# First layer's x: parts split straight from the turned banks, the f32 copy made by GpSimd, idle products dropped, raw turns moved

## The chip, the cores and the metric

The kernel runs on one core of one Trainium2 chip. A core has five engines that work side by side, each through its own queue in order: TensorE (PE, with its weight loads PEld), VectorE (DVE), ScalarE (ACT), GpSimd (POOL) and SyncE (SP, which here only issues DMAs). The metric is device microseconds of one execution, median of three runs. Smaller is better.

## The reference

A decoder trunk of two layers over 16 learned meta tokens and 512 tokens (528 columns), model width 1024, all in f32. Layer 0 is gated linear attention, layer 1 differential softmax attention. Cut to what matters here, layer 0 begins with:

```python
h  = concatenate([meta, x])                 # (528, 1024)
hn = rmsnorm(h, g_norm[0])                  # x * rsqrt(mean(x^2) + eps) * g
proj = hn @ w_in                            # 1024 -> 6160 columns
q, k, v, z, g_lr = split(proj, ...)         # g_lr: 16 columns, rank of the gate
lg = log_sigmoid(g_lr @ w_gate_up + b_gate) / 16
# chunked scan over 64-token chunks with decay exp(cumsum(lg)), then rms, silu(z) gate, w_out
h  = h + y
```

The second layer and a last rmsnorm follow. The change touches only the start of layer 0: how `hn` is put into the form that the products read, and the first product with it, `g_lr`.

## The kernel before, in words

**Number format.** Every large product is done on pairs of fp32r tiles: a value is kept as a high part (ACT copies it with rounding to fp32r) and a low part (DVE subtracts the high part from the value). A product is then three products: high by high, high by low, low by high. `split` (line 274) makes such a pair: line 284 (ACT) and line 285 (DVE).

**Layout.** Activations stand turned: the 1024 model columns are 8 groups of 128 partitions, the tokens lie along the free axis (528: 16 meta, then 512). `X["b11"]` and `b12` hold groups 0 to 3 for the first and second 264 tokens, `X["b21"]` and `X["b22"]` groups 4 to 7. Each is a pair of tiles.

**The prologue.** Token blocks (meta, then four of 128) are loaded, squared and summed (ACT), given their factor (DVE, then POOL for the power -0.5), scaled (DVE, line 723) and turned by TensorE (`turned`, line 743). The scaled turns land in eight PSUM banks, `pts[0]` to `pts[7]`, one for each group k, 512 tokens wide: the first four in the banks named bx, bx, bv, by, the other four in banks of the pool ps, which has four in all. `xm` holds the 16 meta columns, turned and already multiplied by the norm's weight `g_sb`. The unscaled x is turned too (`raw_turn`, line 731, into ps banks) and copied by `raw_copy` (ACT line 737, DVE line 739) to `hT`, the residual stream.

**Making x in the kernel before** (`scaled_pair` and the loop behind it): for groups two at a time, ACT (line 801) and DVE (line 802) each copy one whole bank times `g_sb` to an f32 tile `xg` (named y); POOL puts the meta columns there (line 800). Then `split` makes high and low parts from the f32 tile, 528 columns at a time (two groups of 264). Between them stand the splits of the first two weight tiles wanted by the v products (`ws.make_one`, `kept`, lines 281, 282, 284, 285; wh and wl are a weight's high and low part). The f32 tile is needed later: `token_sums` forms sums and differences of its quarters (x1 to x4) for the seven-product scheme that the later heads use.

**The gate's product**: 32 TensorE products (line 1027) with the 112-column stationary tile `glr`, k by k, into two banks `pgs` (named bx). Ahead of the first ones stand idle products (`warm_up`, line 657, ones by ones into a bank nobody reads); among them stand the turns of raw blocks 3, 4 and 0 and pieces of the first v tile (`W.fill`, line 904). Behind it the gate's rows are copied out (ACT 1044, DVE 1047, ACT 1049, DVE 1052), the up-projection weight is split (ACT 1054, DVE 1055), and then `decay(k)` runs eight times: two products (line 1070) that need both, three ACT steps (1071 to 1073), two DVE steps (1076) and a scan (1077). PE goes on with v and q tiles between the decays.

**What sets the order.** PE's order is the order of the code (a manual schedule) throughout. ACT's and DVE's is the code's until `ordered.close()`; behind that a list scheduler with its own costs puts their instructions in order. Waits between engines are set by the framework from what the instructions read and write. Weight tiles (`raw`) come by SP's DMA queue into two buffers; each transfer waits until the tile two before it has been split.

Of the kernel before, what the change touches and what calls it, by code (L numbers as in the profile page):

```python
# [11 lines left out]
F32 = mybir.dt.float32  # L12
# [3 lines left out]
AF = mybir.ActivationFunctionType  # L16
ALU = mybir.AluOpType
# [3 lines left out]
P = 128  # L21
D = 1024
NM = 16
# [194 lines left out]
def trunk(ctx, tc, x, meta, g_norm, gla_w_in, gla_w_gate_up, gla_b_gate, gla_gnorm, gla_w_out,  # L218
# [21 lines left out]
    def T(p, shape, dt, tag, **kw):  # L240
        uid[0] += 1
        return p.tile(shape, dt, tag=tag, name=f"{tag}_{uid[0]}", **kw)

    def pb_tile(tag):
        return T(pb_pool, [P, 512], F32, tag, bufs=2 if tag == "bx" else 1)
# [7 lines left out]
    def ps_tile():  # L253
        return T(ps_pool, [P, 512], F32, "ps")
# [23 lines left out]
    def split(hi, lo, src, scale=None, keep=False):  # L278

        if keep:  # L280
            act.activation(hi, src, AF.Copy)
            kept.append(lambda: dve.tensor_tensor(lo, src, hi.bitcast(F32), op=ALU.subtract))
        elif scale is None:
            act.activation(hi, src, AF.Copy)  # L284
            return dve.tensor_tensor(lo, src, hi.bitcast(F32), op=ALU.subtract)  # L285
        else:
            act.activation(hi, src, AF.Copy, scale=scale)
            return dve.scalar_tensor_tensor(lo, src, scale, hi.bitcast(F32), op0=ALU.mult, op1=ALU.subtract)
# [365 lines left out]
    def warm_up(n, t=None):  # L654
        t = warm if t is None else t
        for _ in range(n):
            pe.matmul(t[:, :P], ones, ones, start=True, stop=True)
# [83 lines left out]
    def turned(b, ks):  # L741
        for k in ks:
            pe.transpose(pts[k][:, (b - 1) * P:b * P], yt[k // 4][:, b - 1, k % 4 * P:(k % 4 + 1) * P], ident)
# [43 lines left out]

    b12 = x_parts(6)
    xg = []

    def scaled_pair(k0):
        i = k0 // 4
        if k0 % 4 == 0:
            if i == 1:
                for kt in range(4, KT):
                    pts.append(ps_tile())
                    for b in range(1, 5):
                        turned(b, [kt])
            xg.append(T(gp, [P, 4, L], F32, f"y{i}"))
            pool.tensor_copy(xg[i][:, :, :NM], xm[:, 4 * i:4 * i + 4, :])  # L800
        act.activation(xg[i][:, k0 % 4, NM:], pts[k0], AF.Copy, scale=g_sb[:, 0, k0:k0 + 1])
        dve.tensor_scalar(xg[i][:, k0 % 4 + 1, NM:], pts[k0 + 1], g_sb[:, 0, k0 + 1:k0 + 2], None, op0=ALU.mult)

    scaled_pair(0)
    for k0 in range(0, KT, 2):
        if k0 + 2 < KT:
            scaled_pair(k0 + 2)
        i, ks = k0 // 4, slice(k0 % 4, k0 % 4 + 2)
        for n, o in enumerate((X[("b11", "b21")[i]], (b12, X["b22"])[i])):
            split(o[0][:, ks, :], o[1][:, ks, :], xg[i][:, ks, n * HT:(n + 1) * HT])  # L810
        if k0 in (0, 4):
            ws.make_one()
        if k0 == 2:
            kept.pop()()
    ws.held = 0
    x1, x2 = xg[0][:, :, :HT], xg[0][:, :, HT:]
    x3, x4 = xg[1][:, :, :HT], xg[1][:, :, HT:]
# [196 lines left out]
    q_gla_v(0, heads[0])  # L1014
    pgs = pb_pair()
    ws.held = 1
    idle = pb_tile("bv")
    turns_of = {(2, 2): (3, 1), (2, 3): (4, 0), (4, 0): (4, 1)}
    for k in range(KT):
        for n in range(2):  # L1020
            for i, x in enumerate((X["b11"], b12) if k < 4 else (X["b21"], X["b22"])):
                if k == 0:
                    warm_up((3, 3, 1, 4)[2 * n + i], idle)
                if (k, 2 * n + i) in turns_of:
                    b, half = turns_of[k, 2 * n + i]
                    raw_turn(b, [half])
                pe.matmul(pgs[i][:112, :HT], glr[:, k, :], x[n][:, k % 4, :],
                          start=k == 0 and n == 0, stop=k == KT - 1 and n == 1)
        if 1 <= k <= 4:
            W.fill(0.6)  # L1030
        if k == 1:
            raw_turn(3, [0])
        if k == 4:
            raw_turn(0)
        if k == 5:
            for b in (3, 4):
                for i in range(2):
                    raw_copy(b, i, act)
            raw_copy(0, 0, dve)
            raw_copy(0, 1, act)  # L1040
    gh = T(gp, [P, L], F32R, "a0")
    halves = [(pg, slice(i * HT, (i + 1) * HT)) for i, pg in enumerate(pgs)]
    for pg, cs in halves:
# [6 lines left out]
    for pg, cs in halves:  # L1050
        with tc.issue_after(low.ins):
            low = dve.tensor_tensor(gs[32:32 + RANK, cs], pg[32:32 + RANK, :HT], gh[32:32 + RANK, cs].bitcast(F32), op=ALU.subtract)
    wur = T(gp, [P, D], F32R, "z")
    high = act.activation(wur, wup, AF.Copy)
    low = dve.tensor_tensor(wur[64:96], wup[64:96], wur[64:96].bitcast(F32), op=ALU.subtract)
# [27 lines left out]
    for k in range(KT):  # L1083
        decay(k)
        if k == KT - 1:

            tc.mark_branch_hint_location("steep", "LikelyTaken", engines=[
                mybir.EngineType.PE, mybir.EngineType.DVE, mybir.EngineType.Activation, mybir.EngineType.SP])
        W.fill(3.5 if k else 2.0)
        if 1 <= k <= 4:  # L1090
            with behind_gate() if k >= 2 else ExitStack():
                token_sums(k - 1)

    eL = T(hp, [P, KT, 5], F32, "eL")
# [940 lines left out]
```

## Time and profile before

| | |
|---|---|
| median of 3 runs | 964.44 us (964.29 to 965.32) |
| the profiled execution's own time | 964.28 us |
| its span | 962.5 us |
| mean granted TensorE clock | 0.998 |
| PE busy | 952.1 us (99%) |
| DVE busy | 797.0 us (83%) |
| ACT busy | 633.9 us (66%) |
| POOL busy | 82.5 us (9%) |

How to read it: a row of the timeline gives the start in us, how long it took, engine, line of the kernel, operation, output from input, shape and how many in a row; in brackets how long the engine had been idle and who ended that. PE's rows overlap: one product is given some 0.28 us from start to end, while the next starts 0.12 us after it. So PE's pace is read from starts. The same holds in a smaller measure on ACT and DVE, where the next may start some 0.1 us before the end of the one ahead.

### The profile page before, as it was taken

The page shows a single profiled execution, that of the slowest core. Times are in us where ns is not written, and L with a number is a line of the kernel's source. Part 1 is how long each engine was busy: PE and PEld are TensorE (multiplying, and loading weights), DVE is VectorE, ACT ScalarE, POOL GpSimd, SP SyncE. Part 2 cuts the span into 40 slices and gives each one's busy share as a digit, 9 for nine tenths or more (in the row PEclk, how much of TensorE's full clock was granted, in tenths as well). Part 3 has the DMA queues.
Part 4 walks back from the last instruction along what each step waited for, and adds up shares of the span by engine and source line. Part 5 has one row for each costly group of instructions (what it writes and reads, how often), then busy time and mean ns, then how long its engine had stood idle before and what let it go on. Part 6 is the DMA issues. An engine that isn't in the chain of part 4 may idle for free.

```text
span 962.5 us, 18493 instructions
## 1 busy us (share of the span) xinstructions
PE 952.1 (99%) x7173; PEld 911.4 (95%) x7173; DVE 797.0 (83%) x1556; ACT 633.9 (66%) x1311; POOL 82.5 (9%) x167
## 2 busy tenths in 40 slices
PE   9999999999999999999999999999999999999997
PEld 8999999999999999998999898999999999989986
DVE  7989986886878787667997897888889889888875
ACT  8776755477647667657657685585776766755673
POOL 1000000000000100000001121111101101110012
PEclk9999999999999999999999999999999999999999
DMA  8322223634362227234348515234252261523312
GB/s 198 89 83 57 88 67 128 139 114 124 125 166 89 88 94 164 64 110 153 99 105 176 133 56 141 86 122 115 72 166 89 79 160 47 147 90 98 110 45 87
DMA packets 128746, 104.96 MB, mean 109 GB/s; under 512 B 51197, under 2 KB 113181, under 8 KB 128656
## 3 DMA queue, kind: packets, MB, share of 16 engines
q1 hardware_dynamic: 123328, 93.80, 35.4%
q10 hardware_dynamic: 5328, 9.95, 2.9%
q8 instruction: 57, 0.93, 0.4%
q14 instruction: 33, 0.27, 0.1%
HBM read 83.64 MB, written 11.80 MB: 99 GB/s over the span
## 4 chain that ended last, share of the span: by engine, by line
PE 83%; DVE 4%; ACT 1%; DMA 1%; issue 1%; POOL 0%; SPq 0%; POOLq 0%; DVEq 0%
PE bx L441 20%; PE bv L441 12%; PE by L441 11%; PE ps L410 8%; PE bx L998 5%; PE bx L431 4%; PE bx L410 3%; PE bv L998 2%; PE by L998 2%; PE ps L1240 2%; PE bv L410 2%; PE by L410 2%; DMA raw<-in_diff_w_in_dram 1%; PE bv L431 1%; PE by L431 1%; PE ps L1876 1%
## 5 line engine op out<-in xcount | busy, mean ns | idle before, releaser
L285 DVE TENSOR_TENSOR wl<-raw,wh 128x1024 fp32r<-128x1024 f32 x93 | 113.6, 1222 | 20.3 <-ACT wh L284 19.6
L284 ACT ACTIVATE wh<-raw 128x1024 fp32r<-128x1024 f32 x93 | 97.9, 1052 | 39.0 <-PE by L998 22.8
L441 PE MATMUL bv<-x,wh 128*128 128x264 f32 (+1 forms) x736 | 108.9, 285 | 0.0
L441 PE MATMUL bx<-x,wh 128*128 128x264 f32 (+1 forms) x720 | 105.5, 285 | 0.0
L441 PEld LDWEIGHTS bv<-x,wh 128*128 128x128 f32 x736 | 96.8, 188 | 0.9 <-DVE z L498 0.3
L441 PEld LDWEIGHTS bx<-x,wh 128*128 128x128 f32 x720 | 94.4, 188 | 0.5
L285 DVE TENSOR_TENSOR wl<-sum,wh 128x1024 fp32r<-128x1024 f32 x46 | 56.2, 1221 | 10.9 <-ACT wh L284 10.7
L1741 ACT ACTIVATE p<-p,st 128x528 f32<-128x528 f32 (+3 forms) x64 | 36.4, 569 | 40.1 <-DVE st L1739 40.1
L441 PE MATMUL bv<-x,wl 128*128 128x264 f32 (+1 forms) x368 | 62.4, 286 | 0.1
L462 ACT ACTIVATE u<-bx 128x264 f32<-128x264 f32 (+1 forms) x128 | 48.4, 378 | 20.3 <-PE bx L441 17.2
L441 PE MATMUL bx<-x,wl 128*128 128x264 f32 (+1 forms) x360 | 59.0, 284 | 0.0
L284 ACT ACTIVATE wh<-sum 128x1024 fp32r<-128x1024 f32 x46 | 48.4, 1052 | 11.1 <-PE bv L441 5.5
L441 PE MATMUL bx<-x,a11h 128*128 128x264 f32 (+1 forms) x360 | 53.0, 285 | 0.0
L441 PE MATMUL by<-x,a12h 128*128 128x264 f32 (+1 forms) x360 | 52.5, 285 | 0.0
L441 PEld LDWEIGHTS bv<-x,wl 128*128 128x128 f32 x368 | 51.5, 188 | 0.4 <-issue 0.3
L284 ACT ACTIVATE a11h<-raw 128x512 fp32r<-128x512 f32 x46 | 28.9, 628 | 33.8 <-DMA raw<-in_diff_w_in_dram 13.5
L441 PEld LDWEIGHTS bx<-x,wl 128*128 128x128 f32 x360 | 50.0, 189 | 0.3 <-DVE wl L285 0.2
L441 PEld LDWEIGHTS bx<-x,a11h 128*128 128x128 f32 x360 | 47.8, 189 | 0.6
L441 PEld LDWEIGHTS by<-x,a12h 128*128 128x128 f32 x360 | 46.9, 188 | 0.0
L1744 POOL TENSOR_TENSOR st<-st,minus 128x1 f32<-128x1 f32 x32 | 21.4, 670 | 277.4 <-ACT p L1741 225.5
L566 POOL TENSOR_TENSOR st<-st,mhalf 128x1 f32<-128x1 f32 (+1 forms) x20 | 12.1, 606 | 370.3 <-DVE st L565 370.3
L441 PE MATMUL by<-x,a22h 128*128 128x264 f32 (+1 forms) x280 | 40.1, 284 | 0.0
(503 smaller groups left out, 2671.5 us busy)
## 6 DMA issues: line engine op xcount, KB each, us to landing
raw<-in_diff_w_in_dram SPq DMA_DIRECT2D x52, 512.0 KB, 4.8
raw<-in_gla_w_in_dram SPq DMA_DIRECT2D x48, 512.0 KB, 4.2
raw<-in_gla_w_out_dram SPq DMA_DIRECT2D x8, 1024.0 KB, 5.7
raw<-in_diff_w_out_dram SPq DMA_DIRECT2D x8, 1024.0 KB, 5.2
raw<-in_diff_w_in_dram SPq DMA_DIRECT2D x6, 1024.0 KB, 5.9
vd<-planes ACTq DMA_DIRECT2D x12, 268.0 KB, 2.1
vd<-keep ACTq DMA_DIRECT2D x12, 264.0 KB, 2.3
T<-bdr SPq DMA_DIRECT2D x8, 264.0 KB, 3.1
```

The source lines that it names most:

```text
L284: act.activation(hi, src, AF.Copy)
L285: return dve.tensor_tensor(lo, src, hi.bitcast(F32), op=ALU.subtract)
L410: pe.matmul(ps, l, r, start=first and n == 0, stop=last and n == 2, **kw)
L431: pe.matmul(bank, a[:, k, :], b[k] if n0 is None else b[k][:, n0 + i * nn:n0 + (i + 1) * nn], start=n == 0 and ks[0] == 0, stop=n == len(t ...
L441: pe.matmul(bank[:, :x[q].shape[2]], w[p][:, k * P:(k + 1) * P], x[q][:, k, :], start=first and i == 0, stop=i == len(PASSES) - 1, skip_gr ...
L462: W.moved = act.activation(t, self.bx[:, :self.n], AF.Copy, scale=self.sc)
L566: pool.tensor_tensor(dst, dst, mhalf[:np_, :dst.shape[1]], op=ALU.pow)
L998: pe.matmul(banks[i][:, :HT], h.t[p][:, k, mm * P:(mm + 1) * P], s.y[q][k][:, i * HT:(i + 1) * HT], start=n == 0, stop=n == len(PASSES) - 1)
L1240: pe.matmul(o, s.kd[:, i, kc], s.qs[:, i, t0:t0 + n], start=i == 0, stop=i == 1)
L1741: act.activation(p[:, :nk], p[:, :nk], AF.Exp, scale=-1.0, bias=st[:, m:m + 1], accum_out=st[:, 2 + m:3 + m])
L1744: pool.tensor_tensor(st[:, 5:6], st[:, 3:4], minus, op=ALU.pow)
L1876: pe.matmul(ps[i], yp[hd][p][:, k, b * P:(b + 1) * P], wt[q][cs.start // 512][:, 2 * hd + k, cs.start % 512:(cs.stop - 1) % 512 + 1], star ...
```

## The change

- `scaled_pair` and the f32 copy from PSUM go. Groups are taken one by one. For each group k and each half n, ACT makes the high part straight from the bank times `g_sb` (line 803 of the changed kernel, 248 columns for n = 0, 264 for n = 1), and DVE the low part from the bank, `g_sb` and that high part (line 804). The meta columns of both halves' first tiles are split from `xm` ahead of that (two small pairs).
- All turns of groups 4 to 7 stand before that.
- The weight splits stand behind group 3 and behind group 7; before, they stood behind the first, second and third pair of groups.
- The f32 tile is made by POOL as high plus low (line 812), four times 128x4x264.
- The gate's products: the eleven idle products go; k = 0 takes its four in another order; one piece of v work (24 products) behind k = 3; raw block 3's turns behind k = 4 and 5; those of blocks 4 and 0 behind all. Block 3's copies stand ahead of the gate's rows, those of blocks 4 and 0 between the gate's rows and the up-projection split.
- `token_sums(0)` gets the same ordering edge (`behind_gate`) as the others.

```diff
     b12 = x_parts(6)
     xg = []
-
-    def scaled_pair(k0):
-        i = k0 // 4
-        if k0 % 4 == 0:
-            if i == 1:
-                for kt in range(4, KT):
-                    pts.append(ps_tile())
-                    for b in range(1, 5):
-                        turned(b, [kt])
-            xg.append(T(gp, [P, 4, L], F32, f"y{i}"))
-            pool.tensor_copy(xg[i][:, :, :NM], xm[:, 4 * i:4 * i + 4, :])
-        act.activation(xg[i][:, k0 % 4, NM:], pts[k0], AF.Copy, scale=g_sb[:, 0, k0:k0 + 1])
-        dve.tensor_scalar(xg[i][:, k0 % 4 + 1, NM:], pts[k0 + 1], g_sb[:, 0, k0 + 1:k0 + 2], None, op0=ALU.mult)
-
-    scaled_pair(0)
-    for k0 in range(0, KT, 2):
-        if k0 + 2 < KT:
-            scaled_pair(k0 + 2)
-        i, ks = k0 // 4, slice(k0 % 4, k0 % 4 + 2)
-        for n, o in enumerate((X[("b11", "b21")[i]], (b12, X["b22"])[i])):
-            split(o[0][:, ks, :], o[1][:, ks, :], xg[i][:, ks, n * HT:(n + 1) * HT])
-        if k0 in (0, 4):
+    for kt in range(4, KT):
+        pts.append(ps_tile())
+        for b in range(1, 5):
+            turned(b, [kt])
+    x_of = [(X["b11"], b12), (X["b21"], X["b22"])]
+    for i in range(2):
+        hi, lo = [t[:, :, :NM] for t in x_of[i][0]]
+        split(hi, lo, xm[:, 4 * i:4 * i + 4, :])
+    for k in range(KT):
+        g = g_sb[:, 0, k:k + 1]
+        for n, x in enumerate(x_of[k // 4]):
+            hi, lo = [t[:, k % 4, NM * (1 - n):] for t in x]
+            src = pts[k][:, HT - NM:] if n else pts[k][:, :HT - NM]
+            act.activation(hi, src, AF.Copy, scale=g)
+            dve.scalar_tensor_tensor(lo, src, g, hi.bitcast(F32), op0=ALU.mult, op1=ALU.subtract)
+        if k == 3:
             ws.make_one()
-        if k0 == 2:
             kept.pop()()
+        if k % 4 == 3:
+            xg.append(T(gp, [P, 4, L], F32, f"y{k // 4}"))
+            for n in (0, 1) if k == 3 else (1, 0):
+                hi, lo = x_of[k // 4][n]
+                pool.tensor_tensor(xg[-1][:, :, n * HT:(n + 1) * HT], hi.bitcast(F32), lo.bitcast(F32), op=ALU.add)
+    ws.make_one()
     ws.held = 0
...
     ws.held = 1
-    idle = pb_tile("bv")
-    turns_of = {(2, 2): (3, 1), (2, 3): (4, 0), (4, 0): (4, 1)}
     for k in range(KT):
-        for n in range(2):
-            for i, x in enumerate((X["b11"], b12) if k < 4 else (X["b21"], X["b22"])):
-                if k == 0:
-                    warm_up((3, 3, 1, 4)[2 * n + i], idle)
-                if (k, 2 * n + i) in turns_of:
-                    b, half = turns_of[k, 2 * n + i]
-                    raw_turn(b, [half])
-                pe.matmul(pgs[i][:112, :HT], glr[:, k, :], x[n][:, k % 4, :],
-                          start=k == 0 and n == 0, stop=k == KT - 1 and n == 1)
-        if 1 <= k <= 4:
-            W.fill(0.6)
-        if k == 1:
-            raw_turn(3, [0])
-        if k == 4:
-            raw_turn(0)
-        if k == 5:
-            for b in (3, 4):
-                for i in range(2):
-                    raw_copy(b, i, act)
-            raw_copy(0, 0, dve)
-            raw_copy(0, 1, act)
+        for i, n in ((0, 0), (0, 1), (1, 0), (1, 1)) if k == 0 else ((0, 0), (1, 0), (0, 1), (1, 1)):
+            pe.matmul(pgs[i][:112, :HT], glr[:, k, :], x_of[k // 4][i][n][:, k % 4, :],
+                      start=k == 0 and n == 0, stop=k == KT - 1 and n == 1)
+        if k == 3:
+            W.fill(2.6)
+        if k in (4, 5):
+            raw_turn(3, [k - 4])
+    for i in range(2):
+        raw_copy(3, i, act)
+    raw_turn(4)
+    raw_turn(0)
     gh = T(gp, [P, L], F32R, "a0")
...
+    for b in (4, 0):
+        raw_copy(b, 0, act if b else dve)
+        raw_copy(b, 1, act)
     wur = T(gp, [P, D], F32R, "z")
...
         if 1 <= k <= 4:
-            with behind_gate() if k >= 2 else ExitStack():
+            with behind_gate():
                 token_sums(k - 1)
```

How the order moves, at the three places of which the prediction speaks. A row is line, operation, output from input and shape; in square brackets the engines whose progress the instruction waits for (`DVE_49` is VectorE's counter, `PE_49` TensorE's, `Activation_49` ScalarE's). In the names, bx_200, bx_201, bv_202 and by_203 are the banks of groups 0 to 3, x_1_77 and x_34_259 the first and second half's x parts, y_35_260 the f32 tile.

ScalarE where x is made, before:

```order
L801 ACTIVATE y_35_260<-bx_200,g_sb 128x512 [waits DVE_49,PE_49]
L801 ACTIVATE y_35_260<-bv_202,g_sb 128x512
L284 ACTIVATE x_1_77<-y_35_260 128x528 [waits DVE_49,Activation_49,Pool_49]
L284 ACTIVATE x_34_259<-y_35_260 128x528
L281 ACTIVATE wh_270<-raw_133 128x1024 [waits DMAHW0_49]
L801 ACTIVATE y_42_293<-ps_273,g_sb 128x512 [waits PE_49]
```

ScalarE at the same place, with the change:

```order
L284 ACTIVATE x_1_77<-t_242 128x4x16 [waits DVE_49]
L284 ACTIVATE x_2_78<-t_242 128x4x16
L803 ACTIVATE x_1_77<-bx_200,g_sb 128x248 [waits PE_49]
L803 ACTIVATE x_34_259<-bx_200,g_sb 128x264 [waits DVE_49]
L803 ACTIVATE x_1_77<-bx_201,g_sb 128x248 [waits PE_49]
L803 ACTIVATE x_34_259<-bx_201,g_sb 128x264 [waits DVE_49]
L803 ACTIVATE x_1_77<-bv_202,g_sb 128x248 [waits PE_49]
L803 ACTIVATE x_34_259<-bv_202,g_sb 128x264 [waits DVE_49]
L803 ACTIVATE x_1_77<-by_203,g_sb 128x248 [waits PE_49]
L803 ACTIVATE x_34_259<-by_203,g_sb 128x264 [waits DVE_49]
L281 ACTIVATE wh_300<-raw_133 128x1024 [waits DMAHW0_49]
```

In each group the second half's high part now waits for VectorE; what it waits for is the low part of the first half, read from the same bank.

VectorE at that place, with the change:

```order
L804 SCALAR_TENSOR_TENSOR x_1_77<-bx_200,g_sb,x_1_77 128x248 [waits Activation_49]
L804 SCALAR_TENSOR_TENSOR x_34_259<-bx_200,g_sb,x_34_259 128x264 [waits Activation_49]
L804 SCALAR_TENSOR_TENSOR x_1_77<-bx_201,g_sb,x_1_77 128x248 [waits Activation_49]
L804 SCALAR_TENSOR_TENSOR x_34_259<-bx_201,g_sb,x_34_259 128x264 [waits Activation_49]
L804 SCALAR_TENSOR_TENSOR x_1_77<-bv_202,g_sb,x_1_77 128x248 [waits Activation_49]
L804 SCALAR_TENSOR_TENSOR x_34_259<-bv_202,g_sb,x_34_259 128x264 [waits Activation_49]
```

Each low part waits for its high part on ScalarE; before, a pair of groups was handed over at once.

ScalarE between the second weight split and the up-projection's, before (wh_308 is the second weight tile's high part, a the gate's rows, z_435 the up-projection weight):

```order
L284 ACTIVATE wh_308<-raw_133 128x1024 [waits DMAHW1_49]
L284 ACTIVATE x_2_78<-y_42_293 128x528 [waits DVE_49,Activation_49]
L284 ACTIVATE x_3_79<-y_42_293 128x528
L737 ACTIVATE hT_90<-ps_346 128x4x128 [waits PE_49]
L737 ACTIVATE hT_90<-ps_353 128x4x128 [waits PE_49]
L737 ACTIVATE hT_90<-ps_359 128x4x128 [waits PE_49]
L737 ACTIVATE hT_90<-ps_381 128x4x128 [waits PE_49]
L737 ACTIVATE hT_90<-ps_401 128x4x16 [waits PE_49]
L1044 ACTIVATE a_20_159<-bx_316 16x264 [waits PE_49]
```

The same stretch with the change:

```order
L284 ACTIVATE wh_326<-raw_133 128x1024 [waits DMAHW1_49]
L737 ACTIVATE hT_90<-ps_378 128x4x128 [waits PE_49]
L737 ACTIVATE hT_90<-ps_387 128x4x128 [waits PE_49]
L1031 ACTIVATE a_20_159<-bx_330 16x264 [waits PE_49]
L1031 ACTIVATE a_20_159<-bx_331 16x264 [waits PE_49]
L1036 ACTIVATE a_55_422<-bx_330 16x264 [waits DVE_49,Activation_49]
L1036 ACTIVATE a_55_422<-bx_331 16x264 [waits DVE_49]
L737 ACTIVATE hT_90<-ps_402 128x4x128 [waits PE_49]
L737 ACTIVATE hT_90<-ps_407 128x4x128 [waits PE_49]
L737 ACTIVATE hT_90<-ps_417 128x4x16 [waits PE_49]
L1044 ACTIVATE z_437<-v_13_122 128x1024 [waits DMAHW5_49,DMAHW6_49,DMAHW4_49,DMAHW7_49,DMAHW1_49,DMAHW0_49]
```

Two of the raw copies stand ahead of the gate's rows and three behind them, ahead of the up-projection split; before, all five stood ahead of the gate's rows.

## The prediction

> **What bounds the kernel now.** I read the page's busy shares and its chain of work first, then PE's waits, then two stretches, then the timeline of the first 42 us engine by engine.
>
> ```profile
> PE 952.1 (99%) x7173; PEld 911.4 (95%) x7173; DVE 797.0 (83%) x1556; ACT 633.9 (66%) x1311; POOL 82.5 (9%) x167
> PE 83%; DVE 4%; ACT 1%; DMA 1%; issue 1%; POOL 0%; SPq 0%; POOLq 0%; DVEq 0%
> ...
> PE bx L904 <- DVE a L1052: 0.3, 1, 0.3
> PE bx L441 <- DVE ks L881: 0.2, 1, 0.2
> ...
> 33.00:60.00 27.00, 27.00 (x223) 26.73 (x223) 24.49 (x35) 23.35 (x50) 0.00 (x0) 1.00 0.28 79
> 60.00:82.00 22.00, 21.85 (x179) 21.43 (x177) 21.58 (x38) 14.28 (x25) 0.00 (x0) 1.00 0.22 67
> ```
>
> PE is the bound: it works in order, from 33 us on almost without a gap (27.00 of 27 us, 21.85 of 22), and its waits in the whole span are a few tenths. So whatever moves PE's place at 33 us moves the end by nearly as much: later idle time is too small to take up a delay. DVE has 2.5 us to spare between 33 and 60 us and next to nothing between 60 and 82.
>
> The place of the change, on PE:
>
> ```profile
> 13.01 0.44 PE L743 MATMUL bx<-ident,y 128*128 128x128 f32 x2 [0.28 <-DVE y L723]
> 13.50 1.91 PE L743 MATMUL ps<-ident,y 128*128 128x128 f32 x16
> 15.24 0.83 PE L657 MATMUL bv<-ones 128*128 128x128 f32 x6
> 27.00 0.28 PE L904 MATMUL bv<-x,wh 128*128 128x264 f32 x1
> 29.92 0.28 PE L904 MATMUL bx<-x,wh 128*128 128x264 f32 x1
> 30.54 2.09 PE L904 MATMUL bx<-x,wh 128*128 128x264 f32 x15 [0.34 <-DVE a L1052]
> 32.71 0.40 PE L1070 MATMUL ps<-a,z 128*128 128x264 f32 x2
> 41.91 0.41 PE L1070 MATMUL ps<-a,z 128*128 128x264 f32 x2
> ...
> L657 PE MATMUL bv<-ones 128*128 128x128 f32 x22 | 3.0, 275 | 0.0
> ```
>
> The last gate products are issued by 27.00, where the v products begin; 24 products take 2.92 us (27.00 to 29.92, 0.1215 each); the next wants the gate's banks and stalls; the first decay is at 32.71, the third at 41.91. ACT and DVE at that place:
>
> ```profile
> 12.06 1.06 ACT L737 ACTIVATE hT<-ps 128x512 f32<-128x512 f32 x2
> 22.42 2.04 ACT L737 ACTIVATE hT<-ps 128x512 f32<-128x512 f32 x4
> 27.08 0.65 ACT L1044 ACTIVATE a<-bx 16x264 fp32r<-16x264 f32 x2 [1.29 <-PE bx L1027]
> 29.32 0.38 ACT L1049 ACTIVATE a<-bx 16x264 fp32r<-16x264 f32 x1 [0.53 <-DVE a L1047]
> 29.73 1.06 ACT L1054 ACTIVATE z<-v 128x1024 fp32r<-128x1024 f32 x1
> ...
> 23.53 1.32 DVE L285 TENSOR_TENSOR x<-y,x 128x528 fp32r<-128x528 f32 x2
> 24.77 1.25 DVE L822 TENSOR_TENSOR y<-y 128x1056 f32<-128x1056 f32 x1
> 27.50 1.79 DVE L1047 CAST a<-bx 16x264 fp32r<-16x264 f32 x4 [1.34 <-ACT a L1044]
> 30.06 0.42 DVE L1052 TENSOR_TENSOR a<-bx,a 16x264 fp32r<-16x264 f32 x1
> 30.82 1.22 DVE L1055 TENSOR_TENSOR z<-v,z 32x1024 fp32r<-32x1024 f32 x1
> 40.90 0.77 DVE L1076 SCALAR_TENSOR_TENSOR t<-ps,t 128x264 f32<-128x264 f32 x2
> ```
>
> Now the last x part is ready at 24.85 (23.53 + 1.32), ahead of PE's need. The gate's rows run 27.08 to 30.48, the up-projection's low part ends at 32.04 and the first decay follows 0.67 later.
>
> **The change part by part.** *Idle products.* 22 pieces go. Sixteen pieces of that size take 13.50 to 15.24, 0.109 each, so 2.4 us of PE; with the stall at 30.54 (0.62 between two starts where 0.12 is normal) PE could win 2.9 us, if x were ready. It is not.
>
> *The split.* In the changed order each group is a relay over one bank: high part of half 0 (ACT), low part (DVE), then ACT's high part of half 1, which waits for DVE, then DVE's low part. Before, each bank had one reader. The prices:
>
> ```profile
> L801 ACT ACTIVATE y<-ps,g_sb 128x512 f32<-128x512 f32 x2 | 1.4, 688 | 0.0
> L737 ACT ACTIVATE hT<-ps 128x512 f32<-128x512 f32 x7 | 3.7, 587 | 0.0
> 31.76 0.39 ACT L951 ACTIVATE t<-bv 128x264 f32<-128x264 f32 x1
> ...
> 61.21 0.43 DVE L881 SCALAR_TENSOR_TENSOR qs<-bv,t 128x264 f32<-128x264 f32 x1
> 61.56 0.42 DVE L881 SCALAR_TENSOR_TENSOR qs<-by,t 128x264 f32<-128x264 f32 x1
> L422 DVE SCALAR_TENSOR_TENSOR vm<-ps,short,vm 32x128 fp32r<-32x128 f32 x8 | 2.6, 339 | 0.2
> L420 DVE TENSOR_TENSOR am<-ps,am 32x128 fp32r<-32x128 f32 x32 | 9.0, 282 | 1.6 <-ACT am L418 0.5
> L282 DVE TENSOR_TENSOR wl<-raw,wh 128x1024 fp32r<-128x1024 f32 x1 | 1.2, 1219 | 0.0
> ```
>
> A scale read from a tile costs ACT 0.10 (688 against 587), so a high part of 264 takes 0.39 + 0.10, near 0.48, and of 248 near 0.465. On DVE it costs 0.06 (339 against 282): 0.48 and 0.465. DVE starts its next one 0.08 before the end of one (61.21 to 61.56 for 0.43). A hand-over costs 0.03 to 0.04: the gate's copies on DVE end at 29.29 (27.50 + 1.79), and ACT, waiting for them, starts at 29.32. One group then takes: low part 0.465, hand-over 0.04, high part 0.48, hand-over 0.035, low part 0.48 less 0.08. Sum **1.43 us a group**. From below, with neither surcharge, 1.21; with twice the hand-over, 1.5. I take 1.43, since the nearest rows have the surcharges.
>
> The Trainium skill speaks against letting both engines read one bank: "PSUM — Partial Sum Buffer", section "PSUM bank collisions raise a hardware error", says that ScalarE and VectorE must not be in one bank at once, two reads included, and that software has to keep them apart. By that rule the relay cannot be loosened; the order's waits on DVE agree, and the sum by it is the one below.
>
> Start: ACT's raw copies end at 13.12; the two small meta parts follow (64 columns, 0.22 each by the nearest row, quoted below, less the overlap of 0.1), so 13.45; the first bank is turned by then (13.01). The first high part ends at 13.92 and the first low part starts at 13.95; DVE's own small parts fit between. The fourth group's last low part starts at 13.95 + 3 x 1.43 + 1.02 = 19.26 and ends at 19.74. Then the weight: ACT 19.13 to 20.19 (1.06), DVE 20.22 to 21.44, free at 21.36; in the relay's rhythm the fifth group would have begun at 19.67, so the weight adds 1.7. The eighth group's last low part starts at 21.36 + 4.29 + 1.02 = 26.67 and ends at **27.15**, 2.3 later than now.
>
> *PE.* It stands at 15.24 with the gate's products and is led by the relay: some 2.9 us idle before 20.1, then 24 v products to 23.04, then the other gate products and block 3's turns as parts come; the last gate product leaves at 27.3. Turns of blocks 4 and 0 now stand behind it: eight at 0.109 and eight small ones, one of them waiting for block 3's copies; PE takes up v work at 28.9 instead of 27.00, +1.9.
>
> *ACT and the gate's rows.* Its last high part ends at 26.64; the weight's high part runs 26.54 to 27.6, block 3's two copies (0.51 each, 2.04 for four) to 28.6. The gate's rows start at 28.5 instead of 27.08, +1.4. Block 4's two copies and the small one then stand ahead of the up-projection: 1.15 more. Its high part starts at 29.73 + 1.4 + 1.15 = 32.3 and the low part ends at 32.04 + 2.5 = **34.55**. The banks come free at about 31.7 and PE wants them at 31.86, so that stall (0.5) goes. PE's 18 products bring it to 34.05; the decay waits till 34.6. First decay: 34.6 against 32.71, **+1.9**.
>
> *Token sums.* The first (1.25 us on DVE at 24.77) now comes behind the gate. From the up-projection's low part to the second decay's DVE steps there stands as much work as before (32.04 to 40.90, 8.86), because another sum moved behind them: they end near 44.15. PE's third decay needs their banks at 41.91 + 1.9 = 43.8: +0.3. The extra 1.25 is then taken up by DVE's 2.5 spare us before 60; without that cover PE would pay it at 78, where it waits for line 881.
>
> *POOL and the DMAs.* The f32 copies:
>
> ```profile
> 955.18 1.28 POOL L1871 TENSOR_TENSOR t<-keep,x 128x512 f32<-128x512 f32 x1 [2.57 <-DVE keep L1863]
> 955.12 0.42 DVE L1863 TENSOR_TENSOR keep<-keep,ps 128x256 f32<-128x256 f32 x1
> 25.57 0.22 ACT L737 ACTIVATE hT<-ps 128x64 f32<-128x64 f32 x1 [1.11 <-PE ps L731]
> 23.64 0.99 SPq L302 DMA_DIRECT2D raw<-in_gla_w_in_dram  x2
> 39.84 0.99 SPq L302 DMA_DIRECT2D raw<-in_gla_w_in_dram  x2
> ```
>
> 1056 columns at 1.28 for 512 make 2.6 us each: two from 19.8 to 25.0, two from 27.2 to 32.4. DVE's first sum reads the first two at 35.6: ten us of cover. SP's next weight transfer is released by the second weight split, at 28.8 instead of 23.6, and its tile is first split near 46: hidden. The one after it follows the fourth weight split, 2.4 us later than 39.84, and has twenty us.
>
> The sum: +1.9 + 0.3 = **+2.2 us**. On the profiled execution, 964.28 (span 962.5 and 1.78 around it, 0.16 under the median), it gives 966.5; on the median **966.6 us**. A difference of 0.2%, 1.9 us, is about what a measurement of this kernel can tell from none.
>
> **The rivals.** *A lighter relay* (0.26): without the surcharges, 1.21 a group, seven periods x 0.22 = 1.5 less: +0.7, 965.1, within 0.2%. For it: 0.39 and 0.42 are the plain rows; against it: the surcharges are in three pairs of rows. Also here: PE taking back the 0.3 of the third decay.
>
> *The halves run free* (0.08), the other side: ACT's second high part would find VectorE's first low part done, and DVE alone would set the pace, 0.81 a group. The last part is then ready near 22.0, PE never waits more than 0.3, the last gate product leaves at 23.4, and the first decay is 2.7 early; the third decay gives 0.3 back: 962.0. It decides from a period of 1.16 down (1.43 less 1.9/7). Against it: the order has the wait in all eight groups. That is also the case in which the change does what its words say.
>
> *POOL slows DVE* (0.12): the copies run beside both weight low parts (1.22 each), which lie on the relay and ahead of the gate's rows. Were each to take twice as long: +1.2 and +1.2, up to 969.0; one of them, 967.8. Against it: beside POOL's 1.28 above, DVE's 0.42 is its usual time, but that one reads a bank and one tile, not two tiles.
>
> The Trainium skill ("GPSIMD Engine Reference", section "Key points") says that GpSimd shares its SBUF ports with VectorE and contends with instructions that read two SBUF tensors, as the weight low parts do; no row of before shows that pairing at length, so by it this rival rather gains.
>
> *PE's clock falls* (0.06): PE idles 2.9 of the 4.9 us behind 15.24 where the idle products stood.
>
> ```profile
> 1.14 4.64 PE L657 MATMUL ps<-ones 128*128 128x128 f32 x20 [1.14 <-DVE ones L646]
> ```
>
> The first pieces took 0.22 each against 0.109 later. If 24 v products went at half pace, PE would lose 2.9, half of it hidden behind the relay: about 968. Against it: no gap is longer than 1.3 us.
>
> **How the numbers follow.** The forecast has 0.48, with its own range 965.8 to 967.8 (period 1.38 to 1.5 over seven, start 0.25 either way). Slower by over 0.2% takes the forecast's larger part (0.44) and the last two rivals (0.18): 0.62. Within 0.2%: the lighter relay and the forecast's lower edge, 0.29. Faster: 0.09. The range for 8 in 10 goes from the lighter relay, 964.6, to POOL's slowing, 968.7.
>
> **What would show it.** In the changed profile: lines 803 and 804 alternating, each of ACT's second halves idle for DVE, groups 1.4 apart; the last low part ending near 27.2; PE with about 3 us idle between 15.3 and 20.1, waiting for line 804; the gate's rows starting near 28.5, the first decay near 34.6; no stall of 0.3 at the bank's first v product; POOL's four copies of about 2.6 done by 33. A period under 1.2, or a first decay before 33, would prove the sum wrong; weight low parts over 1.3 would speak for POOL, v products 0.2 apart for the clock.

## The result, and the profile after

The changed kernel takes 971.38 us (median of 6 runs, 970.82 to 972.91), the kernel before 964.45 in the same comparison: a ratio of 1.0073 (95% interval 1.0063 to 1.0084), +6.9 us. The forecast was +2.2 us, with a range of 964.6 to 968.7. The direction was right, the size was not, and the time lies above the range.

The page of the changed kernel and its list of waits (us in total, times, longest) show where TensorE lost its place:

```profile
PE 952.5 (98%) x7151; PEld 908.6 (94%) x7151; DVE 800.6 (83%) x1562; ACT 636.6 (66%) x1317; POOL 93.5 (10%) x169
...
PE bx L903 <- DVE a L1039: 2.5, 2, 2.3
PE bx L1018 <- DVE x L804: 1.0, 1, 1.0
```

The wait for line 804 was forecast. The one of 2.3 us for line 1039, the last reader of the gate's banks, was not: it was to vanish. GpSimd is busy 11.0 us longer (93.5 against 82.5).

The small scaling of line 1087 in the kernel before, where it is line 1097:

```profile
29.78 0.17 DVE L1097 TENSOR_SCALAR gn_sb<-gn_sb 128x16 f32<-128x16 f32 x1
```

The timeline of the changed kernel: ScalarE in the split, then VectorE in and behind it, GpSimd, and TensorE:

```profile
16.58 0.48 ACT L803 ACTIVATE x<-bx,g_sb 128x264 fp32r<-128x264 f32 x1 [0.58 <-DVE x L804]
18.01 0.48 ACT L803 ACTIVATE x<-bv,g_sb 128x264 fp32r<-128x264 f32 x1 [0.58 <-DVE x L804]
...
20.90 2.11 DVE L282 TENSOR_TENSOR wl<-raw,wh 128x1024 fp32r<-128x1024 f32 x1 [0.45 <-ACT wh L281]
29.18 2.11 DVE L285 TENSOR_TENSOR wl<-raw,wh 128x1024 fp32r<-128x1024 f32 x1 [0.46 <-ACT wh L284]
31.21 2.43 DVE L1087 TENSOR_SCALAR gn_sb<-gn_sb 128x16 f32<-128x16 f32 x1
33.72 1.79 DVE L1034 CAST a<-bx 16x264 fp32r<-16x264 f32 x4
...
19.48 2.45 POOL L812 TENSOR_TENSOR y<-x 128x1056 f32<-128x1056 f32 x1 [6.28 <-DVE x L804]
21.89 3.45 POOL L812 TENSOR_TENSOR y<-x 128x1056 f32<-128x1056 f32 x1
27.76 2.45 POOL L812 TENSOR_TENSOR y<-x 128x1056 f32<-128x1056 f32 x1 [2.42 <-DVE x L804]
30.15 3.46 POOL L812 TENSOR_TENSOR y<-x 128x1056 f32<-128x1056 f32 x1
...
13.78 0.44 PE L743 MATMUL bx<-ident,y 128*128 128x128 f32 x2 [0.28 <-DVE y L723]
36.03 0.39 PE L903 MATMUL bx<-x,wh 128*128 128x264 f32 x1 [2.27 <-DVE a L1039]
39.41 0.51 PE L1060 MATMUL ps<-a,z 128*128 128x264 f32 x2 [0.41 <-DVE z L1045]
```

Three things are to be seen. The relay is there as worked out: ahead of each second high part ScalarE has stood idle for 0.58 us, waiting for VectorE, and one group follows the other after 1.43 us (16.58 to 18.01). Both weight low parts take 2.11 us where they took 1.22. And a scaling of 16 columns takes 2.43 us, where the same instruction took 0.17 before; the gate's copies queue behind it. GpSimd's rows suggest why: the first copies of the two pairs end at 21.93 and 30.21, the weight low parts end 1.08 later each, and the scaling ends at 33.64, 0.03 after the last copy (33.61). The second copy of each pair is 1.0 longer than the first, as if it waited for VectorE in its turn.

The first decay stands at 39.41 instead of 32.71, +6.70. Of this 0.77 is older than the change: in this execution the last load of x landed later (ScalarE's first work on it starts at 11.13 instead of 10.41), and the last block's turns at line 743 start at 13.78 instead of 13.01.

### The profile page after: what moved, and what is told of

Its sections match the earlier page's. It is cut to its first block, busy times and chain, and to the rows that moved or that the text cites. A ratio compares the mean times of both kernels' runs of the same rounds, so it can differ in the third digit from the quotient of the medians.

```text
span 969.8 us, 18459 instructions
## 1 busy us (share of the span) xinstructions
PE 952.5 (98%) x7151; PEld 908.6 (94%) x7151; DVE 800.6 (83%) x1562; ACT 636.6 (66%) x1317; POOL 93.5 (10%) x169
## 4 chain that ended last, share of the span: by engine, by line
PE 78%; DVE 6%; DMA 2%; issue 2%; ACT 2%; POOL 1%; SPq 0%; DVEq 0%; POOLq 0%; ACTq 0%
PE bx L441 18%; PE bv L441 11%; PE by L441 10%; PE ps L410 8%; PE bx L997 5%; PE bx L431 4%; PE bx L410 3%; PE by L997 2%; PE bv L997 2%; PE ps L1230 2%; PE bv L410 2%; PE by L410 2%; DMA raw<-in_gla_w_in_dram 2%; PE bv L431 1%; PE by L431 1%
```

## The experiments

Ratios are to the kernel before, measured beside each kernel on the same chip.

### Without GpSimd's copies

```diff
-            xg.append(T(gp, [P, 4, L], F32, f"y{k // 4}"))
-            for n in (0, 1) if k == 3 else (1, 0):
-                hi, lo = x_of[k // 4][n]
-                pool.tensor_tensor(xg[-1][:, :, n * HT:(n + 1) * HT], hi.bitcast(F32), lo.bitcast(F32), op=ALU.add)
+            xg.append(yt[k // 4])
+            pool.tensor_copy(xg[-1][:, :, 512:], xm[:, 4 * (k // 4):4 * (k // 4) + 4, :])
```

> The changed kernel without GpSimd's f32 copies; the sums of x further on are taken from other data, so the output is not the reference's, and the order of every other instruction is the same. Theory (GpSimd holds VectorE up): both weight low parts go from 2.11 us back to 1.22, and the small scaling of line 1087 from 2.43 back to 0.17; the first decay comes about 4 us earlier, near 35, and the time is the forecast's, 966.6 us (965.8 to 967.4). Rival (the copies are beside the point; the loss comes from the relay and from raw copies ahead of the up-projection): 970 us or more.

Measured: 967.43 us, ratio 1.0027 (1.0017 to 1.0036). VectorE, ScalarE and TensorE in its timeline:

```profile
20.31 1.23 DVE L282 TENSOR_TENSOR wl<-raw,wh 128x1024 fp32r<-128x1024 f32 x1 [0.45 <-ACT wh L281]
26.76 0.49 DVE L804 SCALAR_TENSOR_TENSOR x<-ps,g_sb,x 128x264 fp32r<-128x264 f32 x1 [0.55 <-ACT x L803]
27.70 1.23 DVE L285 TENSOR_TENSOR wl<-raw,wh 128x1024 fp32r<-128x1024 f32 x1 [0.45 <-ACT wh L284]
28.84 0.17 DVE L1085 TENSOR_SCALAR gn_sb<-gn_sb 128x16 f32<-128x16 f32 x1
33.51 1.22 DVE L1043 TENSOR_TENSOR z<-v,z 32x1024 fp32r<-32x1024 f32 x1 [1.26 <-ACT z L1042]
...
28.52 0.63 ACT L1029 ACTIVATE a<-bx 16x264 fp32r<-16x264 f32 x2
...
13.20 0.44 PE L743 MATMUL bx<-ident,y 128*128 128x128 f32 x2 [0.28 <-DVE y L723]
34.78 0.51 PE L1058 MATMUL ps<-a,z 128*128 128x264 f32 x2 [0.35 <-DVE z L1043]
44.26 0.73 PE L1058 MATMUL ps<-a,z 128*128 128x264 f32 x2
80.91 1.25 PE L441 MATMUL bx<-x,a12h 128*128 128x264 f32 x8 [0.51 <-DVE ks L878]
```

The time is 0.03 above the expected range. VectorE's and ScalarE's instructions there stand in the order of the changed kernel; of GpSimd's work only two small copies of the meta columns are left. The three long rows are short again: 0.88, 0.88 and 2.26 less, together 4.02. The times differ by 3.95 (971.38 to 967.43). So GpSimd's copies cost 4 of the 6.9 us. What is left, +2.8, belongs to what the forecast had counted.

### High parts first, with and without the copies

```diff
-            act.activation(hi, src, AF.Copy, scale=g)
+            parts.append((hi, lo, src))
+        for hi, lo, src in parts:
+            act.activation(hi, src, AF.Copy, scale=g)
+        for hi, lo, src in parts:
             dve.scalar_tensor_tensor(lo, src, g, hi.bitcast(F32), op0=ALU.mult, op1=ALU.subtract)
```

> The changed kernel, but in each group both of ScalarE's high parts stand ahead of both low parts, so ScalarE can be at the next bank while VectorE is at this one. Theory (the relay over one bank makes the 1.43 us period): the period falls to 0.81 to 0.88, the last low part comes about 5 us earlier, near 23.5; GpSimd's copies still slow both weight splits (2.1 us) and still hold line 1087 until one of them ends. 965.4 us if that is the first of the two later copies, 967.6 if it is the second. Rival (what holds the gate up is only GpSimd's last copy): the copies start earlier too, so 966 to 968 as well, but the period stays at 1.4. Rival (two engines that read banks at once slow each other): high and low parts longer than 0.5 each, period over 1.0, time over 969.

> Both edits: high parts first, and no f32 copies (output not the reference's, as in the run without the copies). Theory (relay plus GpSimd make up the whole loss, and dropping the idle products is then a gain): last low part near 22.6, gate's rows from 24.5, first decay near 30.2 against 32.71 before; 962.2 us (961.5 to 963.5). Rival (the raw copies moved ahead of the up-projection and the later token sums cost as much as the earlier x brings): 964 to 965.

Measured: 965.88 us with the copies, ratio 1.0015 (1.0006 to 1.0025); 962.29 without, ratio 0.9972 (0.9961 to 0.9984). VectorE in the run with the copies, then VectorE and TensorE in the run without:

```profile
17.50 3.33 DVE L282 TENSOR_TENSOR wl<-raw,wh 128x1024 fp32r<-128x1024 f32 x1
20.75 3.21 DVE L808 SCALAR_TENSOR_TENSOR x<-ps,g_sb,x 128x248 fp32r<-128x248 f32 x8
23.89 3.29 DVE L285 TENSOR_TENSOR wl<-raw,wh 128x1024 fp32r<-128x1024 f32 x1
```

```profile
19.27 3.22 DVE L808 SCALAR_TENSOR_TENSOR x<-ps,g_sb,x 128x248 fp32r<-128x248 f32 x8
31.03 0.40 PE L1062 MATMUL ps<-a,z 128*128 128x264 f32 x2
```

Eight low parts take 3.21 us, a period of 0.80 a group instead of 1.43: both engines work without a wait, each at another bank. The low parts, which read a bank, are as quick with GpSimd at work (3.21) as without (3.22); the weight low parts, which read two tiles in SBUF, take 3.3 us beside it. That the run with copies came near the expected 965.4 is partly chance: the weights cost 1.2 each more than I had put, and the small scaling no longer stood ahead of the gate's copies there (the scheduler had put it behind them). The run without copies agrees with its sum: 962.2 expected, 962.29 measured, faster than before.

### The kernel before without idle products

```diff
-                if k == 0:
-                    warm_up((3, 3, 1, 4)[2 * n + i], idle)
```

> The kernel before with its idle products dropped and nothing else changed. Theory (TensorE's 2.4 us of idle products stand on the path, the clock does not need them): last gate product near 25.6 instead of 26.9, gate's rows 1.2 us earlier, 963.2 us (962.6 to 964.0). Rival (the last x part at 24.85 leads, the products are covered): no difference, 964.4. Rival (TensorE's pace falls without them): v products over 0.13 us apart and 965 or more.

Measured: 963.41 us, ratio 0.9987 (0.9977 to 0.9996). TensorE:

```profile
26.00 0.28 PE L904 MATMUL bv<-x,wh 128*128 128x264 f32 x1
28.90 2.41 PE L904 MATMUL bx<-x,wh 128*128 128x264 f32 x16
31.39 0.40 PE L1067 MATMUL ps<-a,z 128*128 128x264 f32 x2
```

The last gate products are out and the v products begin at 26.00 instead of 27.00, the first decay comes 1.3 earlier, and the 24 products from 26.00 to 28.90 stay 0.12 apart. The idle products stood on the path, and TensorE's pace does not need them here.

### What holds VectorE: one wait alone, and shorter copies

Two edits of the changed kernel. The first moves the two small scalings behind the gate:

```diff
-    dve.tensor_scalar(gn_sb, gn_sb, 0.5, None, op0=ALU.mult)
+    with behind_gate():
+        dve.tensor_scalar(gn_sb, gn_sb, 0.5, None, op0=ALU.mult)
...
-        dve.tensor_scalar(dgs, dg_sb, -0.5 * (1.0 - LAM_INIT), None, op0=ALU.mult)
+        with behind_gate():
+            dve.tensor_scalar(dgs, dg_sb, -0.5 * (1.0 - LAM_INIT), None, op0=ALU.mult)
```

> The changed kernel with one difference: the two small scalings (lines 1087 and 1121, 128x16 and 128x2) come behind the gate and the up-projection instead of ahead of the gate's copies. GpSimd's copies stay as they are. Theory (VectorE's scaling is held until GpSimd's copy ends, and the gate's copies only queue behind it): the copies of the gate's rows, which read a bank, start at 31.3 instead of 33.7 beside GpSimd; 969.0 us (968.4 to 969.6). Rival (GpSimd holds up whatever VectorE does): the gate's copies start at 33.6 again, 971.4.

The second cuts each of GpSimd's copies into four:

```diff
-                pool.tensor_tensor(xg[-1][:, :, n * HT:(n + 1) * HT], hi.bitcast(F32), lo.bitcast(F32), op=ALU.add)
+                for kk in range(4):
+                    pool.tensor_tensor(xg[-1][:, kk, n * HT:(n + 1) * HT], hi[:, kk, :].bitcast(F32),
+                                       lo[:, kk, :].bitcast(F32), op=ALU.add)
```

> The changed kernel, relay and all, with each of GpSimd's four copies cut into four by groups at the same place: as much work in 16 instructions. Theory (a lock for a whole instruction): each hold is at most 0.6 us instead of 0.9, 0.9 and 2.3: about 968.4 us (967.6 to 969.3). Rival (bandwidth is shared): 971.4, no difference to the changed kernel.

Measured: 969.17 us, ratio 1.0044 (1.0031 to 1.0058), and 967.11 us, ratio 1.0029 (1.0018 to 1.004). VectorE with the scalings moved, then VectorE and GpSimd with the copies cut:

```profile
28.86 2.12 DVE L285 TENSOR_TENSOR wl<-raw,wh 128x1024 fp32r<-128x1024 f32 x1 [0.45 <-ACT wh L284]
31.02 1.79 DVE L1034 CAST a<-bx 16x264 fp32r<-16x264 f32 x4
```

```profile
20.41 1.46 DVE L282 TENSOR_TENSOR wl<-raw,wh 128x1024 fp32r<-128x1024 f32 x1 [0.45 <-ACT wh L281]
28.03 1.46 DVE L285 TENSOR_TENSOR wl<-raw,wh 128x1024 fp32r<-128x1024 f32 x1 [0.46 <-ACT wh L284]
29.41 0.16 DVE L1089 TENSOR_SCALAR gn_sb<-gn_sb 128x16 f32<-128x16 f32 x1
23.37 5.03 POOL L813 TENSOR_TENSOR y<-x 128x264 f32<-128x264 f32 x7 [0.22 <-DVE x L804]
```

With the scalings moved, the gate's copies start right behind the weight low part at 31.02, while GpSimd's last copy still runs (27.45 and 5.87 us for the pair, so to 33.3): the wait of 2.3 us belonged to one instruction of 16 columns, and 2.2 us of time went with it.

With the copies cut, the time is that of the run without any copies within the noise (967.11 against 967.43), and below the expected range. But the cut also moves the work: each piece waits only for its own group, so GpSimd begins at 14.79 and 22.40 instead of 19.48 and 27.76. Its last sums end at 20.79 and 28.40, so only the last 0.4 us of each half's sums runs beside a weight low part, and nothing beside the scaling. The low parts end 1.08 and 1.09 behind the last sum, as they did behind a whole copy, and cost 0.24 more each than alone. That fits a hold, but with so little GpSimd work left beside VectorE this run does not rule out a shared pace. The run by groups below does.

### The hold by itself

> The kernel before with a measurement behind its last output: a row of VectorE instructions (a weight-like difference of two SBUF tiles of 1024 columns, a scaled difference from a bank and a tile, a copy from a bank, a sum of two 16-column pieces, then scalings of 16 and 528 columns and a copy of 512 from one SBUF tile) and a ScalarE copy of 1024 columns, three times: alone, beside GpSimd sums of 1024 columns, and beside GpSimd sums of 128 columns. Its time is some 40 us over the kernel before's and says nothing. Theory (a lock for a whole instruction): beside the long sums each VectorE instruction with two SBUF inputs ends about its own time after a GpSimd sum ends, 1.2 to 3.5 us for the long one, and the next GpSimd sum is longer by that; the scalings and the copy within SBUF are held too; what reads a bank takes its usual 0.4 to 0.5, ScalarE its 1.05. Beside short sums the hold is at most 0.4. Rival (bandwidth is shared): the long difference takes about 2.1 in both, whatever the length of the sums.

The one run took 1025.45 us, 61 more than the kernel before. The rows of VectorE beside GpSimd sums of 1024 columns (2.4 us each), from 975 to 987 us, with one of these sums, and then beside sums of 128 columns, from 996 us:

```profile
976.31 0.43 DVE L2021 SCALAR_TENSOR_TENSOR wl<-ps,wh 128x264 fp32r<-128x264 f32 x1
977.12 1.38 DVE L2023 TENSOR_TENSOR wl<-wh 128x16 f32<-128x16 f32 x1
978.75 2.45 DVE L2027 TENSOR_SCALAR wl<-wh 128x528 f32<-128x528 f32 x1
983.72 2.19 DVE L2026 TENSOR_SCALAR wl<-wh 128x16 f32<-128x16 f32 x1
983.48 2.40 POOL L2033 TENSOR_TENSOR raw<-raw,raw 128x1024 f32<-128x1024 f32 x1
...
996.70 1.50 DVE L2020 TENSOR_TENSOR wl<-raw,wh 128x1024 fp32r<-128x1024 f32 x1
```

What reads a bank keeps its time (0.43, as alone). A scaling or a copy from SBUF to SBUF that comes while a sum runs waits for the end of it: 528 columns take 2.45 us instead of 0.43 alone, 16 columns 2.19 instead of 0.18, and the latter end at 985.91, 0.03 behind the sum (985.88), as the scaling did in the changed kernel. A VectorE sum of two pieces of 16 columns is held in the same way (1.38). Two scalings that came at the border of two GpSimd sums were not held (0.17 at 978.54, 0.43 at 985.95). Beside the short sums the holds are at most 0.3 (1.50 instead of 1.21). The long difference was never caught in the middle of a long sum here: it stood behind the held sum of 16 columns, at the border of two GpSimd instructions. For that case there are the rows of the changed kernel (2.11). ScalarE's copies were done before the loaded stretch, so this run says nothing on ScalarE.

### Both causes taken away, with the whole output

```diff
-        if k % 4 == 3:
-            xg.append(T(gp, [P, 4, L], F32, f"y{k // 4}"))
-            for n in (0, 1) if k == 3 else (1, 0):
-                hi, lo = x_of[k // 4][n]
-                pool.tensor_tensor(xg[-1][:, :, n * HT:(n + 1) * HT], hi.bitcast(F32), lo.bitcast(F32), op=ALU.add)
+        if k % 4 == 0:
+            xg.append(T(gp, [P, 4, L], F32, f"y{k // 4}"))
+        for n, (hi, lo) in enumerate(x_of[k // 4]):
+            pool.tensor_tensor(xg[-1][:, k % 4, n * HT:(n + 1) * HT], hi[:, k % 4, :].bitcast(F32),
+                               lo[:, k % 4, :].bitcast(F32), op=ALU.add)
```

This goes with the high parts first, as above.

> The changed kernel with high parts first, and the f32 copy made by GpSimd group by group, 16 sums of 264 columns, each behind its group's low part; the output is whole. Theory (VectorE waits at most for the sum under way, 0.6 us, and the relay is gone): weight low parts 1.2 to 1.9 us, the rest as in the run without f32 copies: 962.9 us (962.2 to 963.8), faster than before. Rival (bandwidth is shared, 11 us of GpSimd work cost VectorE the same however it is cut): 965 to 966 as with whole copies.

Measured: 962.24 us, ratio 0.9975 (0.9965 to 0.9985), 2.5 us faster than before and some 9 faster than the change as made, and at the lower edge of the expected range. VectorE, GpSimd (all 16 sums together, then two of them singly) and TensorE:

```profile
17.61 1.45 DVE L282 TENSOR_TENSOR wl<-raw,wh 128x1024 fp32r<-128x1024 f32 x1
22.13 1.49 DVE L285 TENSOR_TENSOR wl<-raw,wh 128x1024 fp32r<-128x1024 f32 x1
15.10 13.38 POOL L815 TENSOR_TENSOR y<-x 128x264 f32<-128x264 f32 x16 [2.44 <-DVE x L808]
17.23 0.75 POOL L815 TENSOR_TENSOR y<-x 128x264 f32<-128x264 f32 x1
17.95 1.74 POOL L815 TENSOR_TENSOR y<-x 128x264 f32<-128x264 f32 x1
30.51 0.40 PE L1064 MATMUL ps<-a,z 128*128 128x264 f32 x2
```

GpSimd has work from 15.1 to 28.5 without a pause, so both weight low parts stand wholly beside it, and each loses a quarter of a microsecond. The single sums show how: the sum under way ends at 17.98, the low part ends 1.08 later (19.06), and the next sum takes 1.74 instead of 0.75. In the same order with whole copies the low parts took 3.33 and 3.29. As much GpSimd work beside the same instructions thus costs them only the rest of one sum, so a shared pace is ruled out: it is the length of one instruction that sets the price.

### The first token sum, and the up-projection

In the run without f32 copies and in the run by groups the first token sum's edge to the gate was taken off; in a third kernel the up-projection's split was put ahead of the raw copies of blocks 4 and 0 as well.

```diff
-            with behind_gate():
+            with behind_gate() if k >= 2 else ExitStack():
                 token_sums(k - 1)
```

> The run without f32 copies (relay kept, output not the reference's for the same reason), and the first token sum not held behind the gate; since its data stand from the start there, it is placed early, in VectorE's idle time of the relay. Theory (the sum behind the gate costs what the decays lose after the first: 0.3 by the third, 0.3 at the fourth, 0.3 at the wait for line 881 near 81 us): first decay as before, near 34.8; the later loss goes; 966.6 us (966.2 to 967.1). Rival (that loss has another cause): 967.4, and the decays spread as in the run without f32 copies.

> The run with the copies by group (high parts first, 16 sums by GpSimd), and the first token sum no longer held behind the gate, as in the kernel before; it comes to stand between the second weight split and the gate's copies on VectorE. Theory (held behind the gate it costs 0.7 us, the wait of TensorE at 46 us): that wait goes; the gate's copies come 0.8 later, which reaches the first decay by at most 0.2. 961.8 us (961.2 to 962.4). Rival (the sum ahead of the gate costs as much as behind it): 962.3 or more.

> The run with copies by group and the free token sum, and the up-projection's split ahead of the raw copies of blocks 4 and 0 on ScalarE. Theory (three raw copies ahead of it cost the up-projection 1.15, but TensorE's products cover that when x is early): first decay set by TensorE's products, near 30.5, not by the low part; 961.6 us (961.0 to 962.2), the same as without that edit within 0.3. Rival (the up-projection still sets the first decay): 0.5 or more faster than with the free sum alone.

Measured: 967.66 us, ratio 1.0027 (1.0016 to 1.0037); 962.87, ratio 0.9975 (0.9965 to 0.9986); 963.42, ratio 0.9986 (0.9977 to 0.9995). All three lie above their expected ranges, and none gained, though the mechanism shows in the rows. VectorE and TensorE in the first of them, then TensorE in the second and the third:

```profile
13.91 1.26 DVE L819 TENSOR_TENSOR y<-y 128x1056 f32<-128x1056 f32 x1 [0.30 <-PE bv L743]
36.43 0.40 PE L1058 MATMUL ps<-a,z 128*128 128x264 f32 x2
45.70 0.41 PE L1058 MATMUL ps<-a,z 128*128 128x264 f32 x2
81.70 1.24 PE L441 MATMUL bx<-x,a12h 128*128 128x264 f32 x8 [0.20 <-DVE ks L878]
```

```profile
31.37 0.51 PE L1064 MATMUL ps<-a,z 128*128 128x264 f32 x2 [0.41 <-DVE z L1049]
...
36.06 0.39 PE L1064 MATMUL ps<-a,z 128*128 128x264 f32 x1 [1.12 <-DVE t L1070]
```

From the first decay to the third, and to the wait for line 881 (line 878 in both runs without copies), the kernel before takes 9.20 and 45.17 us (32.71, 41.91, 77.88), the run without copies 9.48 and 46.13 (34.78, 44.26, 80.91), the same with the sum set free 9.27 and 45.27. So the sum behind the gate costs 0.9 later on, as expected. But free it was put ahead of the first low part, at 13.91, and the first decay came 1.65 later: the scheduler gave back more than the edge cost. In the run by groups with the sum set free, TensorE's wait near 46 us (0.74 before) did go, but the first decay came at 31.37 instead of 30.51 (0.31 of this is older: the last block's turns began at 13.54 instead of 13.23), and the time did not fall: there the sum cost as much ahead of the gate as behind it, as the rival said. With the up-projection first, its low part no longer set the first decay; but the scheduler also put another token sum ahead of the first decay's VectorE steps, and TensorE waited 1.12 for them. What the up-projection's place costs by itself stays open; TensorE waits 0.35 for it at the first decay in the run without copies and 0.41 in the run by groups with the free sum, which bounds its price there.

## Why the prediction failed, step by step

- **The relay: right.** The forecast was 1.43 us a group, and 1.43 were measured; the last end, forecast at 27.15, was at 27.25 in the run without copies, whose turns began 0.19 late. That the relay cannot be loosened is true of the order given only: with the high parts first each engine is at another bank, and the period is 0.80.
- **TensorE, ScalarE and the up-projection: right.** The gate's rows were forecast at 28.5 and started at 28.52 in that run; the up-projection's low part was to end at 34.55 and ended at 34.73. The first decay was to come 1.9 later; 34.78 less 32.71 less 0.19 is 1.88. The stall at the bank's first v product was gone there, as forecast, and TensorE waited 0.35 for the up-projection (0.55 forecast).
- **Token sums: sized too small.** The third decay's +0.3 came. But "the extra 1.25 is then taken up" was wrong: 0.7 more was lost between the third decay and the wait for line 881, the place that I had named for the case without cover. The 2.5 us that VectorE has to spare in that stretch are no cover for each decay in it. With the first sum set free, 0.9 came back there. So the forecast's own sum, +2.2, measures +2.8.
- **"POOL and the DMAs": this step failed.** It put GpSimd's copies at nothing. "Ten us of cover" counted when the result is wanted, not what the work does to its neighbours while it runs. The right term is +4.0 us: 0.88, 0.88 and 2.26.
- **The rival had the engine and not the mechanism.** "POOL slows DVE" was held at 0.12 and priced as a pace, twice the length at the weights. It is a hold until the GpSimd instruction under way ends, on VectorE instructions that read two tiles in SBUF or go from SBUF to SBUF, however small. The third and dearest hold was the scaling of line 1087. In the changed kernel it and line 1121 stand ahead of the gate's copies, where before they stood among them; the prediction counted neither.
- What misled me was the row with GpSimd's 1.28 beside VectorE's 0.42: that VectorE instruction read a bank, and in the measurement such instructions are not held. I had written that down as a doubt and still counted the row against the rival. The Trainium skill ("SBUF — State Buffer", section "Who interferes with whom") states the lock: a VectorE instruction with two SBUF inputs, or in a mode that takes both ports, and a GpSimd instruction that reads SBUF block each other for a whole instruction. The trace agrees: VectorE was let in at 21.9 and 30.2, when a copy ended. By that section the sum would have been made with holds of up to the length of one copy (2.45 us as measured) at every such instruction; the section that I had cited only speaks of contention.
- **The clock did not fall.** Without idle products the kernel before is 1.2 us faster, and in the changed kernel the granted clock, the third number from the end in this row of its stretches, is 1.00 where they are gone:

```profile
13.00:23.00 10.00, 8.17 (x57) 6.56 (x55) 7.05 (x15) 5.93 (x14) 3.72 (x3) 1.00 0.85 165
```

- **"The halves run free": right as a mechanism, not in this kernel.** With high parts first the period is 0.80 us (0.81 forecast), and the time 962.29 us without copies (962.0 forecast for this rival).

The loss in the two profiles, added up at the first decay: 0.77 (x landed later) + 1.88 (relay and what follows) + 4.02 (holds) = 6.67 of 6.70. Behind it the changed kernel loses another 0.8 up to the wait for line 881 (line 880 there, at 85.36: 45.95 us against 45.17). Without the 0.77, which is no part of the change, that is 6.7 of the 6.9 us between the medians.

## What to carry to other kernels

When work is given to GpSimd, list every VectorE instruction that will run beside it and read its operands: those that take two SBUF tiles, and scalings and copies from SBUF to SBUF, can be held up to the length of one GpSimd instruction, and so is everything queued behind them; those that read a bank were not held in any row here. Cut GpSimd's work into short instructions (2.45 to 0.75 us here: with high parts first a weight low part beside it went from 3.3 to 1.5 us), and keep small scalings out of the queue ahead of a critical one. When two engines must read one bank, let the first do all its reads of it before the second begins: the same instructions in another order went from 1.43 to 0.80 us a group.

## What was not expected of the hardware

A scaling of 16 columns, 0.17 us alone, took 2.43 us beside one GpSimd instruction, longer than the difference of 1024 columns beside it (2.11). And at the border between two queued GpSimd sums the waiting weight low part was let in both times: the second copy of each pair grew from 2.45 to 3.45 us, so the hold goes both ways.
